# Loading the first two weight units as whole rows, and the first two x parts through one tile

## The chip, the cores and the metric

The kernel runs on one core of one Trainium2 chip. The metric is device time in microseconds (us) for one execution of the whole program; the median of three runs is given. One further execution was recorded by the hardware profiler; all rows of the trace come from that one. Names of the engines: PE is TensorE (matmul), with PEld for its weight loads; DVE is VectorE; ACT is ScalarE; POOL is GpSimd; SP is SyncE, which here only issues transfers. SPq and ACTq are the two engines' transfer issues.

## What is computed

Two layers of a decoder trunk over 256 positions of width 2048, each followed by a LayerNorm of `alpha * x + mixer(x)`. The change touches only the start of the first layer's input projection, `x @ w_in`. Cut to that, with the mixers left out:

```python
def ssd_moba_mixer(x, w_in, conv_w, conv_b, dt_bias, a_log, d_skip, norm_g, w_out):
    z, xbc, dt, q, k, v, gate = jnp.split(x @ w_in, SPLITS0, axis=-1)
    xbc = jax.nn.silu(causal_depthwise_conv(xbc, conv_w, conv_b))
    xs, bm, cm = jnp.split(xbc, (SSD_WIDTH, SSD_WIDTH + SSD_GROUPS * SSD_STATE), axis=-1)
...
def reference(x, in0_w, ...):
    for layer in range(DEPTH):
...
        x = layer_norm(DEEPNORM_ALPHA * x + h, ln_g[layer], ln_b[layer])
    return x
```

`bm` and `cm` are 512 columns each; the kernel computes their projections first.

## The kernel before, in words

**Weights as a stream of units.** All five weight matrices lie in HBM as one list of units of 128 partitions by 1024 floats (512 KB, 4 KB a partition). `split_to` (L217) takes them in order. For each it allocates a tile `raw` (a pool of four), lets SP issue the transfer, and then splits the values in two parts for matmuls in fp32r: ACT copies `raw` to `wh` (rounded), DVE subtracts `wh` from `raw` into `wl`. A product is then formed from three matmuls, `wh` with `xh`, `wh` with `xl`, `wl` with `xh`, where `xh` and `xl` are x split in the same way. `split_to` is called three units ahead of the unit that PE is to use.

**The first two units are special.** A usual unit holds two k tiles (blocks of 128 of the 2048 inner positions) of 512 columns. The layout (L114 to L117) reorders the first two: unit 0 holds k tile 0 for the 512 `b` columns and for the 512 `c` columns, unit 1 the same for k tile 1. So the first matmuls need one k tile of x alone. In `split_to` the branch `n < 2` (L227) loads unit 0 in three transfers of 256, 256 and 512 columns and unit 1 in two of 512 columns, each with its own copy (L236) and subtraction (L238). Ahead of the unit's first piece stands `xpart(n)` (L509): it allocates a tile from the ring `a4` (six buffers), loads k tile n of x (128 KB; n = 0 issued by ACT, n = 1 by SP), and splits it on ACT (L515) and DVE (L519). The `issue_after` lines keep the order on ACT and DVE: x part, then the unit's pieces.

**Order of the transfers on SP**, which issues them one after the other: unit 0 (three), x part 1, unit 1 (two), then x piece 1 (`xpiece`, L494: two k tiles, 256 KB), unit 2, unit 3, x piece 2, unit 4 and so on. The transfer of a unit waits until its buffer `raw` has been read by DVE four units before. Everything that SP issues stands in one queue: what waits there holds up all that follows.

**The first matmuls.** `product_two` (L408) works through the units. For the first two it calls `lead` (L393), which handles the `b` half (n = 0) and the `c` half (n = 1) of the unit: eight matmuls on `wh` and four on `wl` each, of 256 columns, 24 a unit. For the very first half (unit 0, n = 0) the loop in L401 goes over two pairs of column blocks: all three terms of blocks 0 and 1, then of blocks 2 and 3, so that the first 256 columns alone are enough to begin. From unit 2 on `wmm` (L308) issues 24 matmuls a unit. Ahead of it all `warm` (L461) runs eight matmuls on a tile of zeros. PE executes in order, from here to the end of the kernel.

Of the kernel before, what the change touches and what calls it, by code (L numbers as in the profile page):

```python
# [9 lines left out]
F32 = mybir.dt.float32  # L10
# [6 lines left out]
P = 128  # L17
S = 256
# [149 lines left out]
def trunk(tc, io, out):  # L168
    nc = tc.nc
# [3 lines left out]
    def nm(s):  # L173
        count[0] += 1
        return f"{s}_{count[0]}"

    with ExitStack() as top:
# [26 lines left out]
        units = []  # L204
# [5 lines left out]
        loaded = []  # L210
# [6 lines left out]
        def split_to(i):  # L217
            while nsplit[0] <= min(i, len(units) - 1):
                n = nsplit[0]
                if n in early:  # L220
                    with tc.issue_after(loaded[-1].ins):
                        early.pop(n)()
                if n in room:
                    raw = keep[0].tile([P, UK, 512], F32R, tag=room[n], name=nm("raw")).bitcast(F32)
                else:
                    raw = st.tile([P, UK, 512], F32, tag="raw", name=nm("raw"))
                if n < 2:  # L227
                    wh = st.tile([P, UK, 512], F32R, tag="wh", name=nm("wh"))
                    wl = st.tile([P, UK, 512], F32R, tag="wl", name=nm("wl"))
                    for k in range(UK):  # L230
                        if k == 0:
                            xpart(n)
                        for lo, hi in ((0, 256), (256, 512)) if n + k == 0 else ((0, 512),):
                            loaded.append(nc.sync.dma_start(raw[:, k, lo:hi], units[n][:, k * 512 + lo : k * 512 + hi]))
                            with tc.issue_after(conv[-2].ins):
                                conv.append(A.activation(wh[:, k, lo:hi], raw[:, k, lo:hi], AF.Copy))  # L236
                            with tc.issue_after(conv[-2].ins):
                                conv.append(V.tensor_tensor(wl[:, k, lo:hi], raw[:, k, lo:hi], wh[:, k, lo:hi].bitcast(F32), op=OP.subtract))  # L238
                    ready[n] = (wh, wl)
                    nsplit[0] += 1  # L240
                    continue
                loaded.append(nc.sync.dma_start(raw.rearrange("p k n -> p (k n)"), units[n]))
                pool, th, tl = (keep[0], f"wh{n % 8}", f"wl{n % 8}") if n in keep[1] else (st, "wh", "wl")
                wh = pool.tile([P, UK, 512], F32R, tag=th, name=nm("wh"))
                with ExitStack() as pin:
                    if hold[1] is not None:
                        pin.enter_context(tc.issue_after(hold[1]))
                    high = A.activation(wh, raw, AF.Copy)  # L248
                wl = pool.tile([P, UK, 512], F32R, tag=tl, name=nm("wl"))
                with ExitStack() as pin:  # L250
                    if hold[0] is not None:
                        pin.enter_context(tc.issue_after(hold[0]))
                    splits[n] = (loaded[-1], high, V.tensor_tensor(wl, raw, wh.bitcast(F32), op=OP.subtract))  # L253
                ready[n] = (wh, wl)
                nsplit[0] += 1
# [73 lines left out]
        def product(kind, hl, nu=CU, prelude=None, first=WHOLE):  # L329
            ps = banks()  # L330
            for u in range(nu):
                if prelude:
                    prelude(u)
                split_to(unit[0] + 3)
                wpair = ready.pop(unit[0])
                if kind == "w":
                    wmm(ps, u, nu, hl, wpair, first if u == 0 else WHOLE)
                else:
                    last = u == nu - 1
                    steps = [(j, o) for o in range(2) for j in range(UK)] if last else [(j, o) for j in range(UK) for o in range(2)]  # L340
                    for j, o in steps:
                        xmm(ps, o, wpair, j, hl(u * UK + j), u == 0 and j == 0, last and j == UK - 1)
                unit[0] += 1
                pump(nu - 1 - u)
            return ps
# [47 lines left out]
        def lead(pss, at, wpair, hk):  # L393
            (xh, xl, xx), k = hk
            wh, wl = wpair
            for n, ps in enumerate(pss):
                pv = [p.rearrange("p (f n) -> p f n", n=S) for p in ps]
                with ExitStack() as pin:
                    if at or n:
                        pin.enter_context(tc.issue_after(lastmm[-1].ins))  # L400
                    for terms, os in [(t, os) for os in ((range(2), range(2, 4)) if at + n == 0 else (range(4),)) for t in (((wh, xh), (wh, xl)), ((wl, xh),))]:  # L401
                        for o in os:
                            sl = slice(o * P, o * P + P)
                            for i, (l, r) in enumerate(terms):
                                lastmm[:] = [T.matmul(pv[o // 2][:, o % 2, :], l[:, n, sl], r[:, k, :],  # L405
                                                      start=at == 0 and l is wh and i == 0 and o % 2 == 0, stop=False, skip_group_check=True)]
# [59 lines left out]
        def duo(tag):  # L466
            t = big(tag, [P, KT, 2, S], F32R)
            return t[:, :, 0, :], t[:, :, 1, :], t

        xh, xl, xx = duo("A")  # L470
# [10 lines left out]
        with ExitStack() as l0:  # L481
            wk = l0.enter_context(tc.tile_pool(name="wk", bufs=1))
            pp = l0.enter_context(tc.tile_pool(name="pp", bufs=1))

            def a4(shape, dt=F32):
                return wk.tile(shape, dt, tag="a4", bufs=6, name=nm("a4"))
# [20 lines left out]
                early[2 * i if i < PAIRED else PAIRED + i] = xpiece(i)  # L507

            def xpart(k):  # L509
                xr = a4([P, S])  # L510
                (nc.sync if k else nc.scalar).dma_start(xr, io["xt"][:, k, :])
                with ExitStack() as pin:
                    if k:
                        pin.enter_context(tc.issue_after(conv[-2].ins))
                    conv.append(A.activation(xh[:, k, :], xr, AF.Copy))  # L515
                with ExitStack() as pin:
                    if k:
                        pin.enter_context(tc.issue_after(conv[-2].ins))
                    conv.append(V.tensor_tensor(xl[:, k, :], xr, xh[:, k, :].bitcast(F32), op=OP.subtract))  # L519
# [336 lines left out]
            for j in range(4):  # L856
                raw = sz[:, 4 * j : 4 * j + 4, :]
# [384 lines left out]
        with ExitStack() as l1:  # L1242
            wk = l1.enter_context(tc.tile_pool(name="wk1", bufs=2))
# [326 lines left out]
```

## Time and profile before

| | us |
|---|---|
| median of three runs | 1319.52 |
| lowest and highest of them | 1319.34 and 1319.58 |
| the profiled execution, its own time | 1319.45 |
| its span, first to last instruction | 1317.7 |
| PE busy in it | 1309.4 |
| DVE, ACT, POOL busy | 964.5, 695.1, 319.2 |

The span is what the trace shows; 1.75 us of the profiled execution lie outside it. A row of the timeline has the start of an instruction (or of several alike that were merged), its length, the engine, the source line, the operation, the tile that is written and what is read, the count, and in brackets how long the engine had been idle before it and what ended that. An `ACT` row with `<-DMA raw` in the brackets starts at the moment at which the transfer of `raw` had landed.

### The profile page before, as it was taken

The page shows a single profiled execution, that of the slowest core. Times are in us where ns is not written, and L with a number is a line of the kernel's source. Part 1 is how long each engine was busy: PE and PEld are TensorE (multiplying, and loading weights), DVE is VectorE, ACT ScalarE, POOL GpSimd, SP SyncE. Part 2 cuts the span into 40 slices and gives each one's busy share as a digit, 9 for nine tenths or more (in the row PEclk, how much of TensorE's full clock was granted, in tenths as well). Part 3 has the DMA queues.
Part 4 walks back from the last instruction along what each step waited for, and adds up shares of the span by engine and source line. Part 5 has one row for each costly group of instructions (what it writes and reads, how often), then busy time and mean ns, then how long its engine had stood idle before and what let it go on. Part 6 is the DMA issues. An engine that isn't in the chain of part 4 may idle for free.

```text
span 1317.7 us, 21419 instructions
## 1 busy us (share of the span) xinstructions
PE 1309.4 (99%) x7999; PEld 1100.4 (84%) x7999; DVE 964.5 (73%) x1612; ACT 695.1 (53%) x946; POOL 319.2 (24%) x615
## 2 busy tenths in 40 slices
PE   9999999999999999999999999999999999999998
PEld 8988888878888888888888888888888888888886
DVE  6778977775786876777798765859898945555565
ACT  5566668865644554654654444354346544444441
POOL 0044000121036535235787300023232000000000
PEclk9999999999999999999999999999999999999999
DMA  8555566565557667667656868479898765555762
GB/s 316 176 179 180 190 208 194 192 207 176 174 178 234 200 220 231 197 211 221 230 196 232 292 217 320 149 246 333 297 316 290 223 218 190 191 192 187 254 218 78
DMA packets 96126, 288.32 MB, mean 219 GB/s; under 512 B 18482, under 2 KB 28674, under 8 KB 95508
## 3 DMA queue, kind: packets, MB, share of 16 engines
q1 hardware_dynamic: 75796, 245.05, 56.8%
q0 software_dynamic: 6336, 28.35, 6.1%
q10 hardware_dynamic: 13888, 13.54, 3.1%
q8 instruction: 63, 1.03, 0.3%
q14 instruction: 43, 0.35, 0.1%
HBM read 264.35 MB, written 21.00 MB: 217 GB/s over the span
## 4 chain that ended last, share of the span: by engine, by line
PE 99%; DMA 0%; ACT 0%; DVE 0%; SPq 0%; issue 0%
PE main L302 62%; PE main L358 17%; PE main L359 9%; PE main L325 3%; PE aux L455 2%; PE aux L909 1%; PE aux L810 1%; PE enc L1325 1%; PE dec L1370 1%; PE aux L1027 1%; PE aux L995 1%; PE dec L1366 0%; DMA raw<-in_wi 0%; PE main L405 0%; PE turn L455 0%; PE aux L994 0%
## 5 line engine op out<-in xcount | busy, mean ns | idle before, releaser
L253 DVE TENSOR_TENSOR wl<-raw,wh 128x1024 fp32r<-128x1024 f32 x430 | 534.6, 1247 | 285.2 <-ACT wh L248 283.2
L248 ACT ACTIVATE wh<-raw 128x1024 fp32r<-128x1024 f32 x430 | 453.6, 1059 | 481.5 <-PE main L302 261.5
L302 PE MATMUL main<-wh,A 128*128 128x512 f32 x1536 | 488.0, 394 | 0.0
L302 PEld LDWEIGHTS main<-wh,A 128*128 128x128 f32 x1536 | 287.4, 188 | 59.4 <-issue 0.3
L302 PE MATMUL main<-wl,A 128*128 128x512 f32 x768 | 300.6, 391 | 0.0
L358 PE MATMUL main<-A,wh 128*128 128x512 f32 x768 | 272.8, 399 | 0.0
L302 PE MATMUL main<-wh,C 128*128 128x512 f32 x832 | 262.3, 393 | 0.3 <-ACT C L1144 0.3
L359 PE MATMUL main<-A,wl 128*128 128x256 f32 x768 | 215.3, 280 | 0.0
L302 PEld LDWEIGHTS main<-wh,C 128*128 128x128 f32 x832 | 155.7, 188 | 33.8 <-ACT C L1144 0.7
L358 PEld LDWEIGHTS main<-A,wh 128*128 128x128 f32 x768 | 144.2, 188 | 34.9 <-ACT b L882 0.4
L302 PEld LDWEIGHTS main<-wl,A 128*128 128x128 f32 x768 | 144.3, 188 | 28.9 <-issue 0.2
L302 PE MATMUL main<-wl,C 128*128 128x512 f32 x416 | 162.2, 390 | 0.0
L359 PEld LDWEIGHTS main<-A,wl 128*128 128x128 f32 x768 | 145.0, 189 | 0.4 <-issue 0.2
L734 POOL TENSOR_TENSOR c<-c 128x8 f32<-128x8 f32 (+2 forms) x192 | 98.9, 533 | 27.4 <-DMA wb<-c 19.9
L302 PEld LDWEIGHTS main<-wl,C 128*128 128x128 f32 x416 | 78.1, 188 | 16.1
L358 PE MATMUL main<-C,wh 128*128 128x512 f32 x192 | 68.5, 401 | 0.0
L917 POOL TENSOR_TENSOR ssq<-ssq,c 128x256 f32<-128x256 f32 x16 | 18.2, 1137 | 162.5 <-ACT c L915 161.8
L359 PE MATMUL main<-C,wl 128*128 128x256 f32 x192 | 53.7, 281 | 0.0
L968 POOL TENSOR_TENSOR b<-b 128x128 f32<-128x128 f32 x16 | 10.1, 631 | 173.8 <-DVE b L967 171.1
L736 POOL TENSOR_TENSOR c<-c,c 128x4 f32<-128x4 f32 (+2 forms) x96 | 47.3, 493 | 7.4
L737 POOL TENSOR_TENSOR c<-c,c 128x4 f32<-128x4 f32 (+2 forms) x96 | 44.3, 462 | 0.0
L358 PEld LDWEIGHTS main<-C,wh 128*128 128x128 f32 x192 | 36.0, 188 | 8.7
(298 smaller groups left out, 1340.7 us busy)
## 6 DMA issues: line engine op xcount, KB each, us to landing
raw<-in_wi SPq DMA_DIRECT2D x270, 512.0 KB
raw<-in_wo SPq DMA_DIRECT2D x96, 512.0 KB
raw<-in_wglu SPq DMA_DIRECT2D x64, 512.0 KB
wt<-wb POOLq DMA_DIRECT2D x16, 896.0 KB, 7.8
wb<-ob ACTq DMA_DIRECT2D x16, 512.0 KB
b<-cumd SPq DMA_DIRECT2D x16, 256.0 KB
bc<-in_s5bc SPq DMA_DIRECT2D x16, 256.0 KB
wb<-c POOLq DMA_DIRECT2D x16, 256.0 KB, 3.9
```

The source lines that it names most:

```text
L248: high = A.activation(wh, raw, AF.Copy)
L253: splits[n] = (loaded[-1], high, V.tensor_tensor(wl, raw, wh.bitcast(F32), op=OP.subtract))
L302: end = T.matmul(ps[o], l[:, k, sl], r[:, j, :], start=start and i == 0, stop=stop and i == 2)
L325: T.matmul(pv[o // 2][:, o % 2, :], l[:, j, sl], r[:, k, :], start=first and i == 0 and o % 2 == 0, stop=end and i == 2 and o % 2 == 1, sk ...
L358: T.matmul(ps[o], wh[:, j, sl], xx[:, k, :, :].rearrange("p a n -> p (a n)"), start=first, stop=False, skip_group_check=True)
L359: lastmm[:] = [T.matmul(ps[o][:, S : 2 * S], wl[:, j, sl], xh[:, k, :], start=False, stop=end, skip_group_check=True)]
L455: end = T.transpose(dst[:, i * P : i * P + P], s, ident)
L734: G.tensor_tensor(p[:, :, :, 0:m], cs[:, :, :, 1 : m + 1], cs[:, i, :, n : n + 1].unsqueeze(1).to_broadcast([P, 2, 4, m]), op=OP.mult)
L736: G.tensor_tensor(cs[:, 0, :, n + 1 : n + 1 + m], p0[:, 0, :, 0:m], p1[:, 1, :, 0:m], op=OP.subtract)
L737: G.tensor_tensor(cs[:, 1, :, n + 1 : n + 1 + m], p0[:, 1, :, 0:m], p1[:, 0, :, 0:m], op=OP.add)
L810: T.matmul(pk[at : at + 64, 64 * n + a * 16 : 64 * n + a * 16 + 16], d["ev"][:, a, 64 * i : 64 * i + 64], cv[:, a, i, :], start=True, stop ...
L917: G.tensor_tensor(ssq, ssq, jk[:, f, :], op=OP.add)
```

## The change

```diff
                 if n < 2:
                     wh = st.tile([P, UK, 512], F32R, tag="wh", name=nm("wh"))
                     wl = st.tile([P, UK, 512], F32R, tag="wl", name=nm("wl"))
+                    xpart(n)
+                    loaded.append(nc.sync.dma_start(raw.rearrange("p k n -> p (k n)"), units[n]))
                     for k in range(UK):
-                        if k == 0:
-                            xpart(n)
                         for lo, hi in ((0, 256), (256, 512)) if n + k == 0 else ((0, 512),):
-                            loaded.append(nc.sync.dma_start(raw[:, k, lo:hi], units[n][:, k * 512 + lo : k * 512 + hi]))
                             with tc.issue_after(conv[-2].ins):
...
-                    for terms, os in [(t, os) for os in ((range(2), range(2, 4)) if at + n == 0 else (range(4),)) for t in (((wh, xh), (wh, xl)), ((wl, xh),))]:
-                        for o in os:
+                    for terms in (((wh, xh), (wh, xl)), ((wl, xh),)):
+                        for o in range(4):
...
             def xpart(k):
-                xr = a4([P, S])
+                xr = wk.tile([P, S], F32, tag="xfirst", name=nm("xfirst"))
                 (nc.sync if k else nc.scalar).dma_start(xr, io["xt"][:, k, :])
```

Units 0 and 1 are each loaded by one transfer of 128 rows of 4 KB in place of three and two transfers with rows of 1 KB or 2 KB. The copies and subtractions keep their five pieces. The first half of unit 0 is multiplied in the order of the other halves: eight matmuls on `wh`, then four on `wl`. The two x parts no longer take two buffers of `a4`; they share one tile `xfirst` with a single buffer. So the transfer of x part 1, which SP issues, has to wait until ACT (L515) and DVE (L519) have read x part 0, and all transfers that stand behind it on SP (unit 1, x piece 1, units 2 and 3, x piece 2) wait with it.

## The prediction

> **What bounds the kernel now.** I read the page first: the busy shares, then the chain that ended last.
>
> ```profile
> PE 1309.4 (99%) x7999; PEld 1100.4 (84%) x7999; DVE 964.5 (73%) x1612; ACT 695.1 (53%) x946; POOL 319.2 (24%) x615
> ...
> PE 99%; DMA 0%; ACT 0%; DVE 0%; SPq 0%; issue 0%
> ```
>
> PE is the chain. A change at the start is then worth what it moves the point from which PE no longer stops, and it is passed on in full if PE has no idle time later to absorb it. The waits of PE between 7.7 and 1307 us say how much it has:
>
> ```profile
> PE main L302 <- ACT C L1144: 0.3, 1, 0.3
> ```
>
> One wait of 0.3 us in all. So only the first 13 us matter. The timeline of PE there:
>
> ```profile
> 0.99 3.55 PE L464 MATMUL aux<-idle 128*128 128x512 f32 x8 [0.99 <-DVE idle L459]
> 4.66 1.25 PE L405 MATMUL main<-A,wh 128*128 128x256 f32 x8
> 5.74 0.64 PE L405 MATMUL main<-A,wl 128*128 128x256 f32 x4
> 7.62 1.22 PE L405 MATMUL main<-A,wh 128*128 128x256 f32 x8 [1.25 <-ACT wh L236]
> 9.16 1.12 PE L405 MATMUL main<-A,wh 128*128 128x256 f32 x8
> 10.60 1.12 PE L405 MATMUL main<-A,wh 128*128 128x256 f32 x8
> 12.04 1.12 PE L325 MATMUL main<-A,wh 128*128 128x256 f32 x8
> ```
>
> The first half of unit 0 runs from 4.66, then PE waits 1.25 us. From 7.62 it does not stop. Halves start 1.44 us apart (9.16, 10.60, 12.04), a unit takes 2.88 us: unit 1 starts at 9.16, unit 2 at 12.04, units 3 and 4 by the same step at 14.9 and 17.8. If a later version starts unit 1 at 9.16 + d and nothing after it is later than d, the kernel ends d later.
>
> Who sets these starts: ACT and DVE, by what has landed.
>
> ```profile
> 3.88 0.42 ACT L515 ACTIVATE A<-a 128x256 fp32r<-128x256 f32 x1 [1.41 <-DMA a<-in_xt]
> 4.20 0.71 ACT L236 ACTIVATE wh<-raw 128x256 fp32r<-128x256 f32 x2
> 6.94 0.63 ACT L236 ACTIVATE wh<-raw 128x512 fp32r<-128x512 f32 x1 [2.03 <-DMA raw<-in_wi]
> 7.48 0.40 ACT L515 ACTIVATE A<-a 128x256 fp32r<-128x256 f32 x1
> 7.90 1.29 ACT L236 ACTIVATE wh<-raw 128x512 fp32r<-128x512 f32 x2
> 9.49 0.63 ACT L499 ACTIVATE A<-a 128x512 fp32r<-128x512 f32 x1 [0.31 <-DMA a<-in_xt]
> 10.77 1.06 ACT L248 ACTIVATE wh<-raw 128x1024 fp32r<-128x1024 f32 x1 [0.64 <-DMA raw<-in_wi]
> 12.06 1.06 ACT L248 ACTIVATE wh<-raw 128x1024 fp32r<-128x1024 f32 x1 [0.23 <-DMA raw<-in_wi]
> ```
>
> x part 0 has landed at 3.88, the last piece of unit 0 at 6.94, unit 1's first piece by 7.90, x piece 1 by 9.49, unit 2 at 10.77, unit 3 at 12.06. Unit 2 is split by 11.83 and used at 12.04: little slack. And the issues, from the timelines of ACT and SP:
>
> ```profile
> 0.75 0.41 ACTq L511 DMA_DIRECT2D a<-in_xt  x1
> ```
>
> ```profile
> 0.74 1.34 SPq L234 DMA_DIRECT2D raw<-in_wi  x3
> 2.12 0.43 SPq L511 DMA_DIRECT2D a<-in_xt  x1
> 2.60 0.91 SPq L234 DMA_DIRECT2D raw<-in_wi  x2
> 3.54 0.43 SPq L497 DMA_DIRECT2D a<-in_xt  x1
> 4.02 1.01 SPq L242 DMA_DIRECT2D raw<-in_wi  x2
> ...
> 13.11 1.62 SPq L242 DMA_DIRECT2D raw<-in_wi  x2
> ```
>
> Issues follow one another every 0.47 us, and all of the first eight or nine are out before anything big has landed; the transfers then share the queue. In the chain of waits in order of time, the piece that ends PE's wait is one of them:
>
> ```profile
> 1.65 5.27 DMA raw<-in_wi
> ```
>
> 256 KB took 5.27 us from its issue, with others behind it.
>
> **The change part by part.** *Unit 0 in one transfer.* Three issues become one, at 0.74. What a 512 KB transfer takes with little beside it shows at unit 6: issued at 13.11 (the row above), landed at 17.48, 4.37 us.
>
> ```profile
> 17.48 1.06 ACT L248 ACTIVATE wh<-raw 128x1024 fp32r<-128x1024 f32 x1 [0.57 <-DMA raw<-in_wi]
> ```
>
> A transfer quite alone, issued at 260.53, with the DMA view of 260.4 to 264.6 (40 slices of 0.105 us):
>
> ```profile
> 260.53 3.81 SPq L242 DMA_DIRECT2D raw<-in_wi  x2
> ```
>
> ```profile
> GB/s 0 0 0 0 156 0 0 0 0 0 273 117 156 195 78 117 312 351 234 429 234 507 351 351 468 234 273 195 0 39 39 0 39 0 0 0 0 0 0 0
> ```
>
> Its last bytes stand in the 33rd slice, which ends at 263.9: 3.3 us after the issue, some 3.4 with the signal (estimate). So unit 0 lands between 0.74 + 3.4 = 4.1 and 0.74 + 5.27 = 6.0, and I take 4.37, the nearest in size and in queue: 5.1. The first piece went from ACT's 4.20 to PE's 4.66, 0.46 us, so PE begins at about 5.6, and with 24 matmuls in 2.88 us and no 1.25 us gap between the halves it ends unit 0 at 8.5 (before: 9.16). That alone would be a gain of 0.7 us at most. The five pieces on ACT and DVE stay as they are (0.71 and 0.63 us on ACT, hidden behind the matmuls).
>
> *The order of the first twelve matmuls.* Eight and then four, in place of two times four and two. The count is the same; the eighth needs the second 256 columns, which now land with the first and are copied within the 0.71 us above. Cost nothing, covered by ACT being ahead; without that cover one copy, 0.36 us.
>
> *The shared tile.* This is the added wait. x part 1 may be issued when DVE has read x part 0:
>
> ```profile
> 4.33 0.42 DVE L519 TENSOR_TENSOR A<-a,A 128x256 fp32r<-128x256 f32 x1 [3.39 <-ACT A L515]
> ```
>
> That was at 4.75, 0.87 us after the landing at 3.88. In the new order the 1 KB rows of x part 0 share the engines with 4 KB rows, not 1 KB ones; I allow 0.2 us (bounds 0 and 1.0: unit 3 landed 1.29 us after unit 2, so 128 rows of 4 KB take that, and if each of the 128 rows of 1 KB waits for one of them and not for one a quarter as long, it comes 1.0 later). So the release is at 4.97 and x part 1 goes out at 5.0, not at 2.12. Behind it on SP stand unit 1 at 5.47 (before 2.60), x piece 1 at 5.9 (3.54), unit 2 at 6.4 (4.02), unit 3 at 6.9, x piece 2 at 7.3: all 2.3 to 2.9 us later. Unit 4 waited for DVE until 8.32 anyway.
>
> *Unit 1* then lands 4.37 us after 5.47, at 9.84; x part 1, 128 KB, needs what x part 0 needed (0.75 to 3.88, 3.13 us) and is there at 8.1, its copy hidden. From ACT's start on a 512-column piece to PE was 6.94 to 7.62, 0.68 us: PE starts unit 1 at 10.52. Before: 9.16. **d = +1.36 us**, the gain on unit 0 being lost in a wait of 2.0 us (8.5 to 10.5). The bounds: 3.4 us for the transfer gives +0.4; 5.27 us and 0.65 more, since it is twice as long, gives +2.9.
>
> *Unit 2* is next in line. Behind unit 1 come x piece 1 (half of 1.29) and unit 2 (1.29, the step from 10.77 to 12.06): landed at 11.8, split at 12.9, due at 10.52 + 2.88 = 13.4. Not late by more than d. Unit 3 follows 1.3 later with 2.88 to spare. The two `a4` buffers set free save nothing: no wait on them shows.
>
> Sum, on the profiled execution: 1319.45 + 1.36 = 1320.81; the median of the runs is 0.07 above that execution, so **1320.9 us**, less 0.3 at most if the one later wait absorbs some.
>
> [...]
>
> **The rivals.**
>
> *The clock drops (slower).* PE would idle for 2.0 us between the two first units. The clock after thin stretches shows at the end of the trace and in the stretch with the 1.25 us gap:
>
> ```profile
> 4.15:7.56 3.41, 2.11 (x14) 1.52 (x12) 1.09 (x3) 1.38 (x5) 0.00 (x0) 1.00 0.92 258
> ...
> 1308.04:1311.45 3.41, 2.33 (x8) 0.85 (x7) 3.27 (x8) 0.47 (x2) 0.00 (x0) 1.00 0.00 0
> ...
> 1311.45:1317.70 6.25, 1.64 (x3) 0.28 (x1) 1.41 (x2) 1.27 (x2) 0.00 (x0) 0.50 0.46 169
> ```
>
> PE busy 2.11 of 3.41 us kept the granted clock at 1.00; a last stretch with 2.33 us, much of it on two rows alone, was followed by 0.50. In the new kernel 7.56 to 10.97 would hold 0.9 + 0.5 = 1.4 us, less than either. If a half clock followed for one such stretch, PE would lose half of 3.41: +1.7 beside +1.36, **1322.6**. It decides once unit 1 starts after about 10.5. [...]
>
> *The early transfers stay slow (slower).* The 5.27 us for 256 KB may belong to the place, not to the crowd in the queue. Then unit 0 lands at 6.0 or later, unit 1 at 5.47 + 5.27 + 0.65 = 11.4, PE at 12.1: +2.9, **1322.4**. For it: every transfer issued before 4 us took over 5 us except the first three. Against: the queue is empty here when unit 1 is issued.
>
> *Whole rows are quick (faster).* If unit 0 and x part 0 are there by 4.1 and 3.7, and unit 1 by 7.6, PE runs through from 4.6 + 2.88 to about 8.4 and gains 0.8: **1318.7**. This needs unit 1 within 2.3 us of its issue; no row shows less than 3.4.
>
> *The order is not what the diff says.* Were unit 1 put ahead of x part 1 on SP, only x part 1 would be late: landed at 8.1, split by 8.9, PE on unit 1 about 8.8 (its `wh` and `xh` first): -0.4, **1319.1**.
>
> **How the numbers follow.** Forecast 0.49, from +0.4 to +2.6; clock 0.18; slow transfers 0.21; quick rows 0.08; order 0.04. The bound for a difference is 0.2%, 2.6 us, about what a measurement of this kernel can tell from no change: 1316.9 to 1322.2. The forecast lies within it but for 0.03; of the two slow cases 0.34 of 0.39 lie above; the fast ones lie within it but for 0.03, left for what I don't see. So faster 0.03, same 0.60, slower 0.37. The range goes from 1319.1 (the order's case; the quick rows are left out) to 1323.4 (the slow transfers with 1.0 us more for x part 0), leaving out some 0.2.
>
> **What would show it.** In the new trace: SP's issue of x part 1 near 5.0 with a wait on DVE L519; ACT's first piece of unit 0 between 4.2 and 5.2 and no 1.25 us gap between its halves; a wait of PE of about 2 us ahead of unit 1, ended by ACT L236, that one by DMA; unit 2 without a wait; matmul starts still 0.12 us apart at 11 us (0.24 would be the half clock). It would be wrong if PE waits at unit 2 or later, if the rows after 20 us differ by more than the shift, or if x part 1 is issued at once.

## The result, and the profile after

| | before | after |
|---|---|---|
| median, us (17 runs each) | 1320.24 | 1325.34 |
| lowest and highest | 1319.19 and 1324.75 | 1321.57 and 1329.02 |
| the profiled execution, its own time | 1319.45 | 1325.47 |
| its span | 1317.7 | 1323.7 |
| PE starts unit 1, in the trace | 9.16 | 11.50 |

The ratio is 1.0028 with a 95% interval of 1.0017 to 1.004: the changed kernel is slower by 2.2 to 5.3 us. The forecast was 1320.9 and its range ended at 1323.4, so the time lies 1.9 us above the range. A second measurement (changed_again, below) gave 1.0028 once more. Over all runs of this study the changed kernel has a mean of 1324.76 us (29 runs), the kernel before one of 1321.38 (169 runs): 3.4 us more, give or take 0.9. That is the amount to be explained; the 6.0 us between the two spans is that of two single executions.

From the page of the changed kernel, the busy shares and the chain that ended last:

```profile
PE 1309.9 (99%) x7999; PEld 1100.3 (83%) x7999; DVE 964.1 (73%) x1612; ACT 695.3 (53%) x946; POOL 318.3 (24%) x615
...
PE 91%; DMA 5%; DVE 2%; ACT 1%; SPq 1%; issue 1%; ACTq 0%; DVEq 0%
```

PE is busy as long as before (1309.9 against 1309.4 us), but the chain now leaves PE for other engines: there are stops. The view of PE's waits lists them (total, how often, longest):

```profile
PE main L404 <- ACT wh L235: 3.9, 2, 2.6
PE main L301 <- DVE wl L252: 1.1, 1, 1.1
PE dec L1365 <- ACT ys L1375: 1.1, 1, 1.1
...
PE aux L454 <- DVE D L1134: 0.7, 1, 0.7
...
PE enc L1324 <- PE dec L1369: 0.3, 1, 0.3
```

The first row is the start (1.3 us ahead of unit 0, which replaces the old wait inside unit 0, and 2.6 ahead of unit 1). The other four are new and lie far from the edit, at about 713, 837, 979 and 1020 us; they sum to 3.2 us. With the 2.4 us of the start, below, that is 5.6 of the 6.0 us between the two spans; the rest was not located.

**The start.** The timeline of PE in the changed kernel; between 8.24 and 11.50 the second unit is missing:

```profile
0.99 3.40 PE L463 MATMUL aux<-idle 128*128 128x512 f32 x8 [0.99 <-DVE idle L458]
5.71 1.25 PE L404 MATMUL main<-A,wh 128*128 128x256 f32 x8 [1.32 <-ACT wh L235]
...
7.28 1.12 PE L404 MATMUL main<-A,wh 128*128 128x256 f32 x8
8.24 0.64 PE L404 MATMUL main<-A,wl 128*128 128x256 f32 x4
11.50 1.22 PE L404 MATMUL main<-A,wh 128*128 128x256 f32 x8 [2.62 <-ACT wh L235]
```

What SP issued, in its timeline, is not in the program's order:

```profile
0.75 0.87 SPq L231 DMA_DIRECT2D raw<-in_wi  x2
1.66 0.43 SPq L496 DMA_DIRECT2D a<-in_xt  x1
2.13 1.20 SPq L241 DMA_DIRECT2D raw<-in_wi  x2
3.38 0.43 SPq L496 DMA_DIRECT2D a<-in_xt  x1
5.83 0.33 SPq L510 DMA_DIRECT2D xfirst<-in_xt  x1
```

Units 0 and 1 go out together at 0.75, then x piece 1, units 2 and 3 and x piece 2, and only then x part 1 (L510), at 5.83. Nothing waits behind x part 1; x part 1 stands behind everything. (The section on the change says that the transfers behind it wait with it. That is so in the program's text, not in the order of issue that was built from it.) By the records of the transfers unit 1 had landed at 6.07 and x piece 2 at 9.97; in between came 1.57 MB, x pieces 1 and 2 and units 2 and 3, none of which PE could use before x part 1. They kept the transfer engines full, as the windows of this trace show (in each row the stretch and its length, the busy time of PE, PEld, DVE, ACT and POOL, then the granted clock, the share of the transfer engines that was busy, and GB/s):

```profile
9.00:10.40 1.40, 0.00 (x0) 0.00 (x0) 0.00 (x0) 0.41 (x1) 0.00 (x0) 1.00 1.08 404
```

PE does nothing, and 404 GB/s arrive. x part 1 landed at 10.33, 4.5 us after its issue. ACT shows the same:

```profile
4.93 0.42 ACT L514 ACTIVATE A<-xfirst 128x256 fp32r<-128x256 f32 x1 [2.46 <-DMA xfirst<-in_xt]
5.26 1.23 ACT L235 ACTIVATE wh<-raw 128x256 fp32r<-128x256 f32 x3
6.75 0.63 ACT L498 ACTIVATE A<-a 128x512 fp32r<-128x512 f32 x1 [0.26 <-DMA a<-in_xt]
9.99 0.63 ACT L498 ACTIVATE A<-a 128x512 fp32r<-128x512 f32 x1 [2.62 <-DMA a<-in_xt]
10.53 0.40 ACT L514 ACTIVATE A<-xfirst 128x256 fp32r<-128x256 f32 x1
10.84 1.14 ACT L235 ACTIVATE wh<-raw 128x512 fp32r<-128x512 f32 x2
```

Its order was rebuilt in the same way: x pieces 1 and 2 (L498) are copied ahead of x part 1 (L514), and unit 1 (L235) behind that. x part 1 landed at 10.33 and its copy began at 10.53; the copy of unit 1, whose data had been there since 6.07, began behind it at 10.84 and ended PE's wait. Had ACT made that copy in its idle time before 9.99, and had DVE taken x part 1 as early, PE could have begun some 0.5 to 0.7 us sooner (an estimate from these rows). So most of the delay is the transfer, and the order on ACT and DVE has a smaller share. PE starts unit 1 at 11.50 in place of 9.16: +2.34.

### The profile page after: what moved, and what is told of

It reads as the page before. It is cut to its first block, busy times and chain, and to the rows that moved or that the text cites. A ratio compares the mean times of both kernels' runs of the same rounds, so it can differ in the third digit from the quotient of the medians.

```text
span 1323.7 us, 21413 instructions
## 1 busy us (share of the span) xinstructions
PE 1309.9 (99%) x7999; PEld 1100.3 (83%) x7999; DVE 964.1 (73%) x1612; ACT 695.3 (53%) x946; POOL 318.3 (24%) x615
## 3 DMA queue, kind: packets, MB, share of 16 engines
q8 instruction: 63, 1.03, 0.3%
## 4 chain that ended last, share of the span: by engine, by line
PE 91%; DMA 5%; DVE 2%; ACT 1%; SPq 1%; issue 1%; ACTq 0%; DVEq 0%
PE main L301 55%; PE main L357 17%; PE main L358 9%; PE main L324 3%; PE aux L454 2%; DMA yd<-ys 1%; DMA moved<-kt 1%; DMA raw<-in_wo 1%; PE aux L908 1%; ACT wh L247 1%; DMA xr<-in_xn 1%; PE enc L1324 1%; PE aux L994 1%; DMA a<-in_xt 0%; PE dec L1369 0%
## 5 line engine op out<-in xcount | busy, mean ns | idle before, releaser
L733 POOL TENSOR_TENSOR c<-c 128x8 f32<-128x8 f32 (+2 forms) x192 | 93.4, 506 | 18.2 <-DMA wb<-c 10.6
```

The costliest lines, as they stand in the source:

```text
L733: G.tensor_tensor(p[:, :, :, 0:m], cs[:, :, :, 1 : m + 1], cs[:, i, :, n : n + 1].unsqueeze(1).to_broadcast([P, 2, 4, m]), op=OP.mult)
```

## The experiments

Sixteen runs in four groups of four; the kernels of a group ran on one chip beside 35 runs of the kernel before. Its medians there were 1320.36, 1321.26, 1320.74 and 1320.74. In the table "unit 1" is the start of unit 1 on PE in the run's one trace.

| run | median, us | lowest to highest | ratio to before, 95% | unit 1 |
|---|---|---|---|---|
| changed_again | 1323.34 | 1321.84 to 1329.05 | 1.0028 (1.0014 to 1.0043) | 11.61 |
| late_order_restored | 1323.05 | 1321.60 to 1328.25 | 1.0015 (1.0002 to 1.0028) | 11.60 |
| queue_as_written | 1322.38 | 1320.74 to 1327.99 | 1.0016 (1.0003 to 1.0029) | 10.60 |
| two_buffers | 1321.71 | 1318.91 to 1328.17 | 1.0010 (0.9993 to 1.0026) | 8.83 |
| before_again | 1320.64 | 1318.80 to 1326.20 | 0.9997 (0.9982 to 1.0011) | 8.66 |
| late_start | 1324.08 | 1323.17 to 1325.15 | 1.0013 (1.0001 to 1.0025) | 12.80 |
| rows_alone | 1321.23 | 1318.71 to 1327.88 | 1.0005 (0.9987 to 1.0022) | 10.20 |
| tile_alone | 1320.40 | 1320.04 to 1324.16 | 0.9993 (0.998 to 1.0005) | 9.80 |
| rows_and_warmer | 1319.59 | 1318.48 to 1321.72 | 0.9989 (0.9974 to 1.0004) | 8.80 |
| rows_and_pads | 1322.45 | 1318.98 to 1327.50 | 1.0010 (0.9993 to 1.0027) | 10.60 |
| changed_and_pads | 1325.13 | 1322.40 to 1327.12 | 1.0025 (1.001 to 1.0039) | 11.53 |
| before_and_pads | 1322.25 | 1320.27 to 1326.05 | 1.0014 (1.0000 to 1.0029) | 8.66 |
| gpsimd_held | 1322.97 | 1321.45 to 1325.87 | 1.0009 (0.9996 to 1.0022) | 11.55 |
| gpsimd_ahead | 1321.24 | 1318.69 to 1325.61 | 0.9996 (0.9982 to 1.0010) | 8.54 |
| changed_and_warmer | 1324.08 | 1321.78 to 1327.07 | 1.0020 (1.0008 to 1.0031) | 11.76 |
| rows_and_warmer_2 | 1319.38 | 1318.67 to 1323.46 | 0.9986 (0.9974 to 0.9999) | 8.91 |

The 9.16 of the kernel before is that of one trace. Three more traces with its start (before_again, before_and_pads, gpsimd_ahead) have 8.66, 8.66 and 8.54, and the six with the changed start lie between 11.50 and 11.76. By the averages, 8.76 and 11.59, the start is 2.8 us later; 2.34 is the difference of one pair.

The lowest runs are the cleanest reading of the start in the times, since the later waits, which come and go, only add to it: changed kernels with the queue as built begin at 1321.45 to 1322.40, the kernel before, beside each of them, 2.4 to 3.8 us lower (1318.56 to 1319.19).

### The queue on SP, and the later waits

*changed_again*: the changed kernel as it is.

> The changed kernel as it is, on the chip of the three kernels beside it. Theory 1 (the start alone): x part 1 is issued behind x piece 1, units 2 and 3 and x piece 2, PE starts unit 1 at 11.5 us in place of 9.16, and every run is longer by that 2.3 us; what the median showed above it is chance at later places, met by the kernel before as well. Expected +2.3 us, with the lowest runs apart by as much. Theory 2 (the late order): GpSimd issues the load of y (L1394) behind two instructions of the next table, which costs another 1 to 3 us around 950 us; expected +3.5 to +5. Theory 3 (any shift of the start upsets later places): +3.5 to +5 too, at places that differ between profiles.

Unit 1 started at 11.61, and a wait of 1.1 us at 713 stood in this trace too; those at 837 and 979 did not.

*queue_as_written*: the changed kernel, with the order that the prediction assumed held fast on SP.

```diff
+        xdma = []
...
-                    loaded.append(nc.sync.dma_start(raw.rearrange("p k n -> p (k n)"), units[n]))
+                    with ExitStack() as pin:
+                        if n:
+                            pin.enter_context(tc.issue_after(xdma[-1].ins))
+                        loaded.append(nc.sync.dma_start(raw.rearrange("p k n -> p (k n)"), units[n]))
...
-                loaded.append(nc.sync.dma_start(raw.rearrange("p k n -> p (k n)"), units[n]))
+                with ExitStack() as pin:
+                    if n < 4:
+                        pin.enter_context(tc.issue_after(loaded[-1].ins))
+                    loaded.append(nc.sync.dma_start(raw.rearrange("p k n -> p (k n)"), units[n]))
...
-                (nc.sync if k else nc.scalar).dma_start(xr, io["xt"][:, k, :])
+                xdma.append((nc.sync if k else nc.scalar).dma_start(xr, io["xt"][:, k, :]))
```

> The changed kernel with SP's queue held in the order of the program text: unit 0, x part 1, unit 1, x piece 1, unit 2, unit 3. This is the queue that the prediction was worked out for: x part 1 issued at about 5.0 to 5.5 us with unit 1 behind it, PE on unit 1 at 10.5 (bounds 9.6 to 12). It has the late order on GpSimd too. Theory 1: +1.4 us against before. Theory 2: +1.4 and 1 to 3 more. Theory 3: about +1.4 and something more at places that differ.

Its SP timeline has the assumed order; unit 1, which the changed kernel issues right behind unit 0 (both by 1.62), goes out at 6.21 here, behind x part 1:

```profile
5.82 0.34 SPq L517 DMA_DIRECT2D xfirst<-in_xt  x1
6.21 0.42 SPq L235 DMA_DIRECT2D raw<-in_wi  x1
```

And ACT and PE in it:

```profile
8.06 0.42 ACT L521 ACTIVATE A<-xfirst 128x256 fp32r<-128x256 f32 x1 [1.58 <-DMA xfirst<-in_xt]
9.91 1.16 ACT L239 ACTIVATE wh<-raw 128x512 fp32r<-128x512 f32 x2 [1.44 <-DMA raw<-in_wi]
```

```profile
5.70 2.08 PE L411 MATMUL main<-A,wh 128*128 128x256 f32 x8 [0.92 <-ACT wh L239]
...
10.60 1.21 PE L411 MATMUL main<-A,wh 128*128 128x256 f32 x8
```

With nothing ahead of it in the queue x part 1 needs 2.2 us from its issue (5.82 to 8.06), against 4.5 behind the others. Unit 1 is the last to come, as predicted: landed at 9.91, on PE 0.69 us later. (That PE shows no wait there is because unit 0 ran slowly in this execution, 2.08 us for eight matmuls, and ended at the same moment; more on this under rows_alone.) The start is 10.60, so the order that was actually built costs a further 0.9 us.

*two_buffers*: the changed kernel, `xfirst` with two buffers, so that x part 1 waits for nothing.

```diff
-                xr = wk.tile([P, S], F32, tag="xfirst", name=nm("xfirst"))
+                xr = wk.tile([P, S], F32, tag="xfirst", bufs=2, name=nm("xfirst"))
```

> The changed kernel with two buffers for xfirst, so that x part 1 waits for nothing: whole rows alone. Order on all engines as before the change apart from the five loads that became two. Unit 0 lands at about 5.0, x part 1 and unit 1 by 6.5, PE starts unit 0 at 5.5 and goes from half to half without a wait: unit 1 at about 8.5, in place of 9.16. Theory 1: -0.6 us against before. Theory 2: the same. Theory 3: -0.6 with later places upset as much as in the changed kernel, so 0 to +2.

PE in it goes from unit 0 to unit 1 without a stop:

```profile
5.83 1.25 PE L404 MATMUL main<-A,wh 128*128 128x256 f32 x8 [1.06 <-ACT wh L235]
...
8.83 1.12 PE L404 MATMUL main<-A,wh 128*128 128x256 f32 x8
```

With a free x part 1 the late start is gone: unit 1 starts 0.33 us sooner than in the one trace of the kernel before that the prediction read, and 0.2 to 0.3 us later than in its other traces. The lowest run is 1318.91. Without the shared buffer there is no late start. The median of 1321.71 is not clearly above that of the kernel before; its trace has a 3.0 us wait at 975, which is taken up below.

*late_order_restored*: besides the start, the changed program differs from the one before in one place: on GpSimd the load of `y5` (L1394, at about 950 us) now stands behind the small table of block 7 (L1314 and L1315). Here it is put back.

```diff
-                    G.memset(rt[:, :, 0:1], 0.0)
+                    with ExitStack() as pin:
+                        if b == 7:
+                            pin.enter_context(tc.issue_after(after["y"].ins))
+                        G.memset(rt[:, :, 0:1], 0.0)
...
-                nc.gpsimd.dma_start(y5[j], yd[j].rearrange("g a c -> (g a c)").rearrange("(f p t) -> p f t", p=P, t=S))
+                after["y"] = nc.gpsimd.dma_start(y5[j], yd[j].rearrange("g a c -> (g a c)").rearrange("(f p t) -> p f t", p=P, t=S))
```

> The changed kernel, with GpSimd's load of y put ahead of the table of block 7 again, as it was before the change. Theory 1: the same as the changed kernel within 0.5 us, start of unit 1 at 11.5 us. Theory 2: 1 to 3 us faster than the changed kernel, +2.3 us against the kernel before. Theory 3: the same as the changed kernel.

It did not lower the time beyond what the spread of the runs allows (1323.05 beside 1323.34), and the wait at 978 was 1.5 us in its trace, no smaller than with the order that it undoes (1.1 and none). The times alone could not tell 1 us from nothing here (standard errors of the two means: 0.6 and 0.7 us), but the wait that the late order was to make stayed, so nothing speaks for it as the cause.

### The parts alone

*before_again* is the kernel before, *late_start* the same with 27 warming matmuls in place of 8 (`WARM0 = 27`), so that PE is late and all transfers are as before.

> The kernel before as a run of its own, for a second profile and for a test of the comparison. Theory 1: ratio 1.000; its own profile may show a wait at one of the later places where the changed kernel's first profile had them (713, 837 and 977 us), since they are chance. Theory 3: ratio 1.000 and none of these waits.

> The kernel before with 27 matmuls on zeros ahead in place of 8, so that PE starts unit 0 at about 8.5 us and unit 1 at 11.4 to 11.5, as late as in the changed kernel, while all transfers and their order stay as before (the scheduler puts GpSimd's load of y late here too). Theory 1: +2.3 us. Theory 2: +3.5 to +5, with the late order. Theory 3: +3.5 to +5, since the shift is the same.

before_again had a wait of 1.1 us at 975 in its trace (1318.9 us of span against 1317.7): the kernel before also has such waits, only not in the execution that the prediction read. late_start came out 3.64 us late at unit 1, more than wanted; its lowest run is 4.5 us above the lowest of before, its median 2.8. A late start alone raises the floor, and what chance adds on top is not the same from kernel to kernel (0.9 us from lowest to median here, 2.6 for the kernel before on that chip).

*rows_alone* is the kernel before with the whole-row lines of the diff; *tile_alone* the kernel before with the `xfirst` line alone.

> The kernel before with the whole rows alone: units 0 and 1 in one transfer each, x parts in two buffers of a4, the first half of unit 0 in its old order. Theory 1: PE on unit 0 at 5.7 to 5.8 and without a wait on to unit 1 at 8.7, -0.4 us against before; the same as the kernel with two buffers for xfirst. Theory 3: -0.4 and up to +1.5 from later places.

> The kernel before with the shared tile alone: five transfers for units 0 and 1, x part 1 waiting for x part 0's readers. The scheduler puts x part 1 behind unit 1 and x piece 1 on SP, not behind units 2 and 3. It is issued at about 4.8 and lands at 9.5 to 10 behind what is in the queue; PE starts unit 1 at 10.5, +1.3 us; units 2 and 3 are issued after it, at 5.2 and 5.7, and unit 2 must not be later than 13.4. Theory 1: +1.3 to +2. Theories 2 and 3: 1 to 3 us more. If the tile costs as much as the whole change, +2.3, the rows have no part in it.

In tile_alone unit 1 starts at 9.80, +0.64: there x part 1 goes out at 4.80, ahead of units 2 and 3, and the pieces of unit 0 let PE begin at 4.68. The time is not different from before. So the two parts together lose what neither loses alone: with both, x part 1 is put behind units 2 and 3, with the tile alone it is not. What in the building of the order decides that was not tried. In rows_alone PE shows another effect:

```profile
0.99 3.78 PE L463 MATMUL aux<-idle 128*128 128x512 f32 x8 [0.99 <-DVE idle L458]
5.80 2.08 PE L404 MATMUL main<-A,wh 128*128 128x256 f32 x8 [1.03 <-ACT wh L235]
...
10.20 1.12 PE L404 MATMUL main<-A,wh 128*128 128x256 f32 x8
```

Eight matmuls took 2.08 us, where two_buffers had 1.25: unit 0 ran slowly for the most part (0.23 us from matmul to matmul, against 0.12 from 10.20 on) and took 4.4 us instead of 3.0. Its last four, from 9.72, took the 0.64 us of two_buffers. Whole rows leave PE idle for about 1 us between the warming matmuls and unit 0 (here 4.77 to 5.80). PE worked 2.55 of the 3.42 us from 2.22 to 5.64 and 3.25 of the 3.41 us up to 9.05. two_buffers was idle for 1.06 us there and had the quick unit 0, so the gap alone does not decide it; what does is not shown.

*rows_and_warmer*: rows_alone with `WARM0 = 12`, which fills most of that gap. *rows_and_warmer_2* is the same kernel again, in the last group.

> Whole rows alone, with 12 matmuls on zeros ahead in place of 8, so that PE is not idle between them and unit 0 at 5.7 us. In the profiles of whole rows the granted clock came at 5.3 us once and at 9.1 once, and unit 1 started at 8.8 and 10.2: with the late clock unit 0 runs at half speed. If the idle stretch after the warm-up is what delays the clock, it is granted by 7.5 us here, unit 1 starts at 8.7 to 9.2 in every run, and the slower runs lose 1 us. If the phase alone decides, unit 1 starts anywhere from 8.8 to 10.2 as before. Theory 1 for the rest: lowest run within 0.3 us of the lowest of before.

> The kernel before with whole rows for both units and 12 warming matmuls, as in rows_and_warmer, to be measured again beside the others: unit 1 at 8.8 us, a median of 1319.5 to 1320, ratio 0.998 to 1.000, and every run of the unchanged start lower than the changed kernel's by 2.5 us or more in the lowest runs. Rival: its mean of 1319.9 was chance, and it comes out at the 1321 us of the kernel before.

```profile
0.99 4.41 PE L463 MATMUL aux<-idle 128*128 128x512 f32 x12 [0.99 <-DVE idle L458]
5.79 1.25 PE L404 MATMUL main<-A,wh 128*128 128x256 f32 x8 [0.39 <-ACT wh L235]
...
8.80 1.12 PE L404 MATMUL main<-A,wh 128*128 128x256 f32 x8
```

In the first of the two PE is idle for 0.39 us ahead of unit 0 in place of 1.03, the first eight matmuls take 1.25 us and unit 1 starts at 8.80. Over both runs (24 executions) the median is 1319.38 and the mean 1319.94, 1.4 below the mean of the kernel before; the second ratio, 0.9986, excludes 1 by a hair, the first does not. This is the best version found, by about 0.1%. The gain does not come from unit 1, though, which starts no sooner than in the kernel before (8.80 and 8.91, against 8.54 to 9.16). The two traces have no later wait above 0.3 us; why these runs have fewer of them is not shown.

### Semaphore numbers

With whole rows three transfers fall away at the start, and the numbering of the transfers' semaphores is shifted by three in the rest of the program. Three tiny loads (of 2 rows of 8 floats) restore it in rows_and_pads and changed_and_pads; before_and_pads has five of them, which shifts the kernel before.

```diff
...
+                    if i == 2:
+                        for q in range(3):
+                            with tc.issue_after(xdma.ins):
+                                xdma = nc.sync.dma_start(pads[q], io["lnr"][0:2, 8 * q : 8 * q + 8])
```

> Whole rows alone, with three tiny loads of 64 bytes added on SP after x piece 2, where SP is idle, so that all later transfers get the same of the eight completion semaphores as in the kernel before. Everything else as in whole rows alone. Theory 4 (the numbering of the semaphores upsets later places): the spread falls to that of the kernel before, mean -0.3 us against it. Theory 3, or chance: spread and mean as in whole rows alone, mean about +1.

> The changed kernel with the same three tiny loads. Theory 4: mean +2.5 us against before, the start alone, and a narrow spread. Otherwise as the changed kernel, mean +3.4 to +4.2 us, with single runs up to 7 us above the lowest.

> The kernel before with five tiny loads, which puts all later transfers on the semaphores that they have in the changed kernel (five and three are the same modulo eight, the other way round). Start as before (unit 1 at 8.7 to 9.2). Theory 4: mean 1 to 2 us above before, spread as in the changed kernel. Otherwise ratio 1.000.

With the numbers put back changed_and_pads stays at 1.0025, and rows_and_pads is within the interval of rows_alone, so the numbers do not make the changed kernel slow. before_and_pads is at 1.0014 (1.0000 to 1.0029), its mean 1.2 us above that of the kernel before, which is what theory 4 asked for; its trace has a wait of 4.1 us at the place of two_buffers' 3.0. Whether the numbers, the five loads themselves or chance made that is open.

### GpSimd and the wait at 713

By now a wait of PE for DVE's `wl` at about 713 us stood in four traces of four that had the changed start (after, changed_again, late_order_restored, changed_and_pads; 0.8 to 1.1 us) and in rows_alone (1.6). The chain of waits of the changed kernel ahead of it, in order of time:

```profile
699.85 6.31 DMA moved<-kt
...
709.77 0.83 DVE ob L790
710.60 0.60 DVE tm L791
...
713.36 1.15 DVE wl L252
...
714.55 1.66 PE main L301 x6
```

DVE is what PE waits for, and DVE is slow. The same instruction of 256 elements, L790, in the DVE timeline of the changed kernel and beside it GpSimd's, which runs a loop of its own there (`phasors`, L725 to L738; its operations grow from 8 to 248 elements a round):

```profile
709.77 0.83 DVE L790 TENSOR_TENSOR ob<-bc,lap 128x256 f32<-128x256 f32 x1
710.53 0.68 DVE L791 TENSOR_TENSOR tm<-bc,lap 128x256 f32<-128x256 f32 x1
```

```profile
699.84 0.58 POOL L738 DMA_DIRECT2D wb<-c  x1 [0.30 <-POOL c L736]
...
708.15 2.18 POOL L733 TENSOR_TENSOR c<-c 128x248 f32<-128x248 f32 x2
...
711.81 0.59 POOL L738 DMA_DIRECT2D wb<-c  x1 [0.30 <-POOL c L736]
```

The kernel before, DVE at the same lines (L791 there is L790 here) and GpSimd's end of the round:

```profile
706.43 0.43 DVE L791 TENSOR_TENSOR ob<-bc,lap 128x256 f32<-128x256 f32 x1
706.78 0.42 DVE L792 TENSOR_TENSOR tm<-bc,lap 128x256 f32<-128x256 f32 x1
```

```profile
701.51 0.58 POOL L739 DMA_DIRECT2D wb<-c  x1 [0.30 <-POOL c L737]
...
707.34 0.45 POOL L734 TENSOR_TENSOR c<-c 128x16 f32<-128x16 f32 x2
```

In the changed kernel PE is 2.4 us later here than before and DVE 3.3 us (709.77 against 706.43), while GpSimd is 1.7 us earlier (699.84 against 701.51): its loop does not move with PE, and its long operations now meet DVE's. In all five traces with the wait the round after that one ends between 711.2 and 713.4; in the nine others measured by then, of which one has a wait of 0.3 us there, it ends between 717.5 and 722.3. To see whether that is the cause, *gpsimd_held* delays one round of the loop in the changed kernel, by repeating two small copies:

```diff
-                for i in range(2):
-                    G.tensor_copy(cs[:, i, :, 1], phi[:, i, sl])
+                for i in range(2 * (12 if b == 13 else 1)):
+                    G.tensor_copy(cs[:, i % 2, :, 1], phi[:, i % 2, sl])
```

> The changed kernel; in the fourteenth of the sixteen rounds of the phasor loop on GpSimd (L728) two small copies are repeated eleven times more, some 3.5 us by 0.16 us each, with the same result; the two DMAs of `c` that went out at 699.8 and 711.8 should go out at about 703.5 and 718. Theory: the wait of 1.1 to 1.5 us at about 713, which stood in all four profiles of the changed kernel's start, comes from GpSimd running ahead of PE there, its operations of 128 and 248 elements slowing DVE (0.67 to 0.84 us where 0.42 us was usual). Then the wait is gone, the same DVE instructions take 0.42 us, and the times lie about 1.4 us lower: median about 1323, mean ratio about 1.0015. Rival: the wait belongs to the late start itself (weights, order of PE); then it stays at 1.1 to 1.5 us. Unit 1 still starts at 11.5.

DVE in gpsimd_held:

```profile
710.41 0.43 DVE L790 TENSOR_TENSOR ob<-bc,lap 128x256 f32<-128x256 f32 x1
710.76 0.41 DVE L791 TENSOR_TENSOR tm<-bc,lap 128x256 f32<-128x256 f32 x1
```

GpSimd's two DMAs went out at 707.40 and 722.58, the instructions are back at 0.42 us, the wait at 713 is gone, and unit 1 started at 11.55 as in the changed kernel. (The delay is twice the planned one, and not all of it need be the edit's: in late_start, without the edit, the DMAs went out at 705.23 and 722.30. PE is 1.5 us later here as well, by a drop of the clock that is told below.) The mean of the runs is 1323.23, 1.5 us below the changed kernel's 1324.76 (standard errors 0.3 and 0.4), the standard deviation 1.1 us against 2.3; the two were measured in different groups. All eighteen traces fit: at least two of the three DVE instructions take 0.67 to 0.84 us in each of the five with the wait, and none takes over 0.52 in the other thirteen. So in these traces the wait goes with GpSimd's place beside DVE.

*gpsimd_ahead* was to make it in the kernel before, with four buffers in the ring of the loop (`tag="c2", bufs=4`).

> The kernel before, with four buffers in place of three in the ring `c2`, so that the phasor loop on GpSimd waits less for its DMA and runs further ahead. The start is as before (unit 1 at 8.7 to 9.2). Theory: GpSimd ahead of PE makes the wait at about 710 to 713; DVE's instructions of 256 elements there take 0.67 us or more, and a wait of PE of 1 us or more appears in a kernel whose start is not late: mean ratio 1.0005 to 1.001. Rival: no wait there without a late start; ratio 1.000.

It missed its aim. The loop ran a whole round ahead (its DMAs at 691.93, 704.57 and 718.60), so that the quiet part of a round lay beside L791 again; DVE took 0.42 us and no wait came. It says nothing on the theory.

*changed_and_warmer*: the changed kernel with `WARM0 = 12`.

> The changed kernel with 12 warming matmuls in place of 8. The granted clock should be full at about 4 us, as in rows_and_warmer, and not at 10 us. Theory: unit 1 waits for x part 1 in any case, so it still starts at about 11.5 us, and the time is that of the changed kernel, 1323 to 1325. Rival: the late clock is part of the loss; then the time falls by 1 us or more.

Unit 1 started at 11.76 and the time, 1324.08, is the changed kernel's: unit 0 was done at 9.68, and PE then waited 2.07 us. How fast unit 0 ran did not count while x part 1 was missing: its first eight matmuls took 1.50 us here and 2.07 in changed_again, where unit 1 started at 11.61. Its trace is, beside that of gpsimd_held, the only one with the changed start and no wait at 713; GpSimd's DMAs were at 701.04 and 717.72. So the wait is frequent with the changed start (four of five, gpsimd_held not counted), not certain. late_start and queue_as_written, whose PE is late as well, do not have it.

## Why the prediction was wrong

**Unit 0 and the order of its matmuls: right.** Forecast were a start at 5.6 and an end at 8.5; the trace has 5.71 and 8.72 (the second half begins at 7.28, twelve matmuls 0.12 us apart). The order of the first twelve matmuls costs nothing: unit 0 takes 3.00 us with it (5.83 to 8.83 in two_buffers) and 3.01 with the old order (5.79 to 8.80 in rows_and_warmer). Not foreseen were the idle time ahead of unit 0 (1.32 us here) and the slow matmuls that stood behind such a gap in rows_alone (2.08 us for eight); with the changed start the wait for x part 1 covers them (2.07 us in changed_again, unit 1 at 11.61). The start at 5.71 hangs on x part 0 too, and there a term was too small: the prediction allowed it 0.2 us more than before, with 1.0 as the bound, and it landed at 4.91 in place of 3.88. So DVE had read it at 5.80, and x part 1 went out at 5.83, not at 5.0.

**The shared tile: the step that failed.** "Behind it on SP stand unit 1 at 5.47 (before 2.60), x piece 1 at 5.9 (3.54)": the working took the program's order as SP's order. Where that order holds the sum comes out: queue_as_written starts unit 1 at 10.60, forecast 10.52. That it fits to 0.1 us is luck, as two errors cancel: unit 1 went out at 6.21 and not at 5.47, since x part 0 was late, and took 3.70 us and not 4.37. But SP issued everything that could go and put x part 1 last, and x part 1 then stood behind 1.6 MB. d was +2.34, not +1.36.

**The rival "the order is not what the diff says"** had the mechanism and the wrong price, -0.4. It let x part 1 land at 8.1, 3.1 us after its issue, as if nothing stood ahead of it. So placed the transfer takes 2.2 us (queue_as_written); behind units 1 to 3 and both x pieces it took 4.5 and landed at 10.33. The rival also had ACT copy unit 1 ahead of x part 1, and ACT copied it behind. The transfer moved to the end of the queue had to be charged with the bytes ahead of it: the 1.57 MB that landed between 6.07 and 9.97, at 403 GB/s, as the window row has it.

**"So only the first 13 us matter": the second step that failed.** One execution was read, and it had no later wait. The kernel before has them too: before_again shows one of 1.1 us in 1318.9 us of span, and 169 runs have a median of 1320.61 beside the 1319.52 of the three. And the shift of PE was not passed on unchanged where another engine kept its own pace: the wait at 713 goes with the place of GpSimd beside DVE (0.83 us for an instruction that takes 0.43 in the kernel before). The sum over both: the start, 2.34 and 0.1 more by unit 2; at 713, 1.2 us (a gap of 1.45 us from matmul to matmul, where 0.23 is usual) in four of five executions, 1.0 on average; 3.4 us together, the difference of the means, if the other waits are alike in both. So close a fit is chance: with the start averaged over the traces (2.8 us) the sum is 3.9, also within the 3.4 give or take 0.9, and late_start, with PE 3.64 us late, has a mean only 2.4 us above the kernel before. The waits at 837 and 979 of the profiled execution are not part of this: they come and go in both kernels.

**The rival "the clock drops"** did not happen in the profiled execution, but in gpsimd_held it did. The windows of gpsimd_held, then one of the changed kernel (columns as above):

```profile
8.74:12.15 3.41, 0.74 (x7) 0.60 (x6) 1.45 (x3) 2.11 (x5) 0.00 (x0) 1.00 0.65 248
12.15:15.57 3.42, 3.42 (x19) 3.42 (x18) 3.35 (x5) 2.71 (x3) 0.00 (x0) 0.50 0.47 178
```

```profile
7.23:10.65 3.42, 1.65 (x14) 1.45 (x13) 0.69 (x1) 0.80 (x3) 0.00 (x0) 1.00 1.04 405
```

In gpsimd_held a stretch of 3.41 us with 0.74 us of work was followed by 3.42 us at half clock; in the changed kernel one of 3.42 us with 1.65 us of work was not (the clock stayed at 1.00 up to 14.06). Why the one and not the other is not shown. The half clock cost 1.5 us (unit 2 began 4.47 us after unit 1, against 2.98 in the changed kernel's profile), near the 1.7 that the rival named, but on top of the start, and not in every execution: the first eight matmuls of unit 1 took 1.60 us in gpsimd_held and 1.22 or 1.23 in four others with that start (after, changed_again, late_order_restored, changed_and_warmer). Late in two_buffers 4.00 us with 0.96 us of work (974 to 978) were followed by 3.40 us at 0.51. At the end of the kernel before, as the prediction shows, a stretch with 2.33 us of work, much of it on two rows, was followed by 0.50.

**The other two rivals.** Early transfers were not slow by their place: unit 0, issued at 0.75, landed at 4.74, and in queue_as_written unit 1 took 3.7 us (6.21 to 9.91). Whole rows were quick for unit 1, which was there at 6.07 where this rival asked for 7.6, since it was issued at once; unit 0, landed at 4.74, missed the 4.1 that it asked for. With x part 1 free (two_buffers) unit 1 starts at 8.83, not at 8.4, and the kernel before starts it at 8.54 to 8.66 in three of four traces: no gain of whole rows at the start is shown.

## What to carry to other kernels

When an edit adds a wait to a transfer, ask which order of issue will be built around it: it may be the waiting transfer that goes to the back, and then its price is the bytes that were let ahead of it (here 4.5 us from issue to landing in place of 2.2). Read more than one execution before a later wait is called absent, and look for engines that run at their own pace beside the one that is shifted. Look also at the speed of the first real matmuls: behind an idle 1.03 us eight of them took 2.08 us in rows_alone, and 1.25 us in rows_and_warmer, where four more warming matmuls had left 0.39 us of it.

## What was not expected of the hardware

*The first matmuls run at two speeds.* With whole rows and eight warming matmuls the first eight matmuls of unit 0 took 2.07 or 2.08 us in four traces (changed_again, late_order_restored, queue_as_written, rows_alone) and 1.25 in three (after, two_buffers, gpsimd_held). before_again, with the old loads, had 2.08 too, and the first trace of that kernel 1.25. The slow ones are near what the half clock gives: in the stretch of gpsimd_held with a granted clock of 0.50 eight such matmuls took 1.91 us. With x part 1 free or early unit 0 took 3.0 us in the quick case (two_buffers) and 4.4 (rows_alone) or 4.9 us (queue_as_written) in the slow one. The PE work in some 3.41 us ahead of unit 0 or up to its start was 2.83 us in the changed kernel (0.41 to 3.82) and 3.00 in rows_and_warmer (0.58 to 3.99), both with 1.25 us for the first eight, and 2.55 in rows_alone (2.22 to 5.64), with 2.08. What decides between the two speeds is not shown. Full clock was also lost later on: 0.74 us of work in 3.41 us was followed by 0.50 in gpsimd_held, as told above.

*DVE beside GpSimd.* The same instruction of 256 elements took 0.42 or 0.43 us beside GpSimd operations of up to 16 elements (before, 706.43 to 707.54) and 0.67 to 0.83 beside those of 124 and 248 (after, 709.77 to 711.79).

*One transfer goes with much of the spread.* In two_buffers PE waits 3.0 us for `ys`, and the chain of waits leads back to a transfer to HBM issued at 959.89:

```profile
959.89 16.22 DMA yd<-ys
```

In the changed kernel's profile it took 14.87 us and PE waited 1.1. In the kernel before it was issued at 958.91, ACT, which waits for it, went on at 969.99, 11.1 us later, and PE did not wait. Over the eighteen traces PE waited at this place in ten (0.6 to 4.1 us) and not in the other eight. From the 49th matmul of the projection to the end of the execution these eight take 1307.0 to 1309.5 us, the five with a wait above 2 us 1311.1 to 1314.3. Behind the 3.0 us the granted clock was 0.51 for 3.4 us; a window of two_buffers:

```profile
978.00:981.40 3.40, 3.40 (x83) 3.09 (x84) 2.54 (x3) 2.99 (x4) 0.00 (x0) 0.51 0.13 24
```

Open stays why this transfer takes 11 us in one trace and 16 in another, why the kernels differ so much in their spread (lowest to highest 2.0 us in late_start, 9.3 in two_buffers), and what sets the pace of GpSimd's loop from one execution to the next.
